# The second pass of the attention scores as two 64-row products on the two halves of the array, in the first half's attention

## The chip, the cores and the metric

The kernel runs on one core of one Trainium2 chip. The metric is the device time of one execution in microseconds; smaller is better. The profile is one execution of the same program, recorded by the hardware profiler.

## The reference

A backbone of two layers over 1024 latent tokens and 256 context tokens, with 1024 features, all in float32. Layer 0 mixes tokens by a convolution module, layer 1 by attention with 16 query heads, 4 key heads and 64 dimensions per head; each is followed by a SwiGLU feed-forward. The part that the change touches:

```python
def gqa_sdpa(q, k, v):
    B, Q, H, Dh = q.shape
    qg = q.reshape(B, Q, N_KV_HEADS, KV_GROUP, Dh)
    s = jnp.einsum("bqkgd,bskd->bkgqs", qg, k).astype(jnp.float32) * (Dh ** -0.5)
    p = jax.nn.softmax(s, axis=-1).astype(v.dtype)
    o = jnp.einsum("bkgqs,bskd->bqkgd", p, v)
    return o.reshape(B, Q, H * Dh)
```

There are 1280 keys (1024 latent and 256 context tokens) and 1024 queries.

## The kernel before

The kernel is one instruction stream per engine, in an order that a scheduler makes from the program's order, its priorities and its tiles. Products run on TensorE in the type float32r, which keeps fewer bits than float32. To keep accuracy, operands are split in two: a high part, rounded to float32r, and a low part, the rest. A projection then takes three products per block (`mm3`, L172 to L174: high by high, high by low, low by high). A weight is split when it is loaded (`wload`, a ScalarE cast and a subtraction).

Attention works in units: one key head t and 128 queries, so four query heads share the keys. 16 units are the first half's attention (queries 0 to 511) and 16 the second's. The first half begins beside the rest of the query projections, then runs alone; the second half runs beside the output projection and the feed-forward.

- `load_q` brings a unit's q from DRAM, where the projections left it, into one of two places of the tile q, on GpSimd's queue (POOL). Its 128 rows are the 64 dimensions of the high part and below them the 64 of the low part. It is called for the next unit when a unit begins.
- `load_k` brings the keys of a head: row block 0 to 63 and row block 64 to 127 hold the same keys; columns 0 to 1279 hold their high part and columns 1280 to 2559 their low part. Heads 0 and 2 lie in the tile KB, heads 1 and 3 in the tile T3 (in `order` rows T_12365).
- `scores` computes, for each of the four query heads, 128 queries by 1280 keys in PSUM. The 1280 columns fall on three banks of 512 columns, as pieces of 512, 512 and 256 (in that order or with the 256 first). Each piece takes two passes of all 128 rows (L1012): (high + low of q) by high of k, then (high + low of q) by low of k, added up in the bank. VectorE scales the piece of 1280 columns and finds its extreme (L1018), ScalarE takes the exponential (L1020).
- `values` transposes the weights by TensorE (L1030), splits them (L1033 on ScalarE, L1034 on VectorE), and multiplies by the values (L1036, L1037), for ten blocks of 128 keys; four more transposes (L1051) bring the sums into place for the division. The weights of one unit are worked on while the scores of the next are made.
- `attn_stream` interleaves the two, and `attention` sets the banks: `sring` says where in PSUM the next head's scores go, one place while projections run beside, two places in turn when attention runs alone.

Scores for a head are followed in program order by some blocks of the unit before; the scheduler moves single products apart from their neighbours where it expects waits, so that the last pieces of a head can stand twenty and more instructions behind the first.

Of the kernel before, what the change touches and what calls it, by code (L numbers as in the profile page):

```python
# [8 lines left out]
F32 = mybir.dt.float32  # L9
F32R = mybir.dt.float32r  # L10
# [5 lines left out]
P = 128  # L16
# [4 lines left out]
TOK = CTX + SEQ  # L21
# [3 lines left out]
NH, NKV, HD = 16, 4, 64  # L25
# [30 lines left out]
class Kern:  # L56
# [936 lines left out]
    def load_q(self, t, qt):  # L993
        nc = self.nc
        self.qi += 1
        q = self.qroom[:, self.qi % 2 * 512:self.qi % 2 * 512 + 512]
        q = q.rearrange("p (h t) -> p h t", h=4)
        nc.gpsimd.dma_start(q, self.qsd[t].rearrange("(r h) t -> r h t", h=4)[:, :, qt * P:(qt + 1) * P])
        return q.bitcast(F32R)

    def scores(self, q, rq, kt, slots, Ps, sums):

        nc = self.nc
        for h in range(4):
            o = self.sring[self.si % len(self.sring)]
            self.si += 1
            sc = self.ps.rearrange("p b n -> p (b n)")[:, o:o + TOK]
            k0 = 0
            while k0 < TOK:
                w = min(512 - (o + k0) % 512, TOK - k0)  # L1010
                for p in range(2):
                    nc.tensor.matmul(sc[:, k0:k0 + w], lhsT=q[:, h, :], rhs=kt[:, p * TOK + k0:p * TOK + k0 + w],  # L1012
                                     start=p == 0, stop=p == 1)
                k0 += w

            mn = self.sp.tile([P, 8], F32, tag="mn", name="mn", bufs=4)[:, 0:1]
            pt = slots[h]
            nc.vector.tensor_scalar(out=pt, in0=sc, scalar1=rq[:, h:h + 1], scalar2=None, op0=ALU.mult, op1=ALU.min,  # L1018
                                    accum_out=mn)
            nc.scalar.activation(pt, pt, AF.Exp, bias=mn, scale=-1.0, accum_out=sums[:, 0, h:h + 1])  # L1020
            Ps.append(pt)
            yield 1.07
# [276 lines left out]

    def attention(self, final, qr):  # L1300
        nc, a, c = self.nc, self.a, self.c
        kbuf = self.T("T3", [P, 2 * TOK], F32R)
        pr1 = self.T("T1", [P, 3, TOK])
        prh = self.T("HS", [P, 4, TOK])
        ptt = self.T("T2", [P, 4, 2, 512], F32R)
# [1 line left out]
        self.ptslot = self.si = self.qi = 0  # L1307
        del self.raws[2:]
        self.qroom = self.room()
        units = [(t, q) for t in range(NKV) for q in range(4)]  # L1310
        self.olast = self.cp.tile([P, 2, P], F32, tag="olast", name="olast")

        def dst(q0):
            def of(t, q):
                if (t, q % 4) == (NKV - 1, 3):
                    return self.olast, lambda: None
                st = self.sb(256).rearrange("p (a q) -> p a q", q=P)

                def done():
                    nc.gpsimd.dma_start(self.od[:, 2 * t:2 * t + 2, q * P:(q + 1) * P], st)  # L1320
                return st, done
            return of
# [9 lines left out]
        self.lav = 40  # L1332
        self.bgq.append(qr)
        pr4 = None
        for us in self.attn_stream(units, (self.kub, kbuf), dst(0), True):
            if self.bgq:
                self.pump(self.rate * us)
            elif pr4 is None:
                pr4 = self.T("T5", [P, 3, TOK])
                self.pring = self.pring[:4] + [pr4[:, 0], pr4[:, 1], pr4[:, 2]] + self.pring[4:]  # L1340
                self.set_banks(**alone)
                self.sring = [0, TOK]
        self.lav = 40

        self.lo_dve = 1.0
        self.set_banks(mm=[6], st=[6], pt=[5], av=[7])
# [116 lines left out]
        for us in self.ffn(1, [(fR[0], 512)], ("T1",), ("HS",), (zR,), parts=2, tail=(first, second)):  # L1463
# [3 lines left out]
            if len(zR) == 1 and not end:  # L1467
# [3 lines left out]
                for j in range(2):  # L1471
                    nc.tensor.matmul(s0[:, j:j + 1], lhsT=yacc[:, j * P:(j + 1) * P], rhs=c["ones"],
                                     start=True, stop=True)
# [100 lines left out]
```

## Time and profile before

| what | value |
|---|---|
| median of 3 runs | 2965.94 us (2965.63 to 2966.03) |
| span of the profiled execution, first to last instruction | 2962.1 us |
| time of that execution outside its span | not on the page; the runs' median is 3.8 us above the span |
| TensorE busy | 2881.8 us, 97% |
| VectorE busy | 1917.6 us, 65% |
| ScalarE busy | 1210.5 us, 41% |
| score products (L1012), both halves | 768 |
| first half's attention | 1578.8 to 1855.0 us |

How to read it: PE is TensorE's products and PEld its weight loads, which run beside products; DVE is VectorE, ACT is ScalarE, POOL is GpSimd. A product's record is longer than its share of TensorE's time, because its modelled end includes the way through the array, where the next product already follows; the distance from start to start is what it costs in a row of products. A row of the order of time has the start and the length in us, engine, line, operation, out<-in, rows*columns of the weights, and rows x columns of the result. A window row has its length, then each engine's busy time and instructions, TensorE's granted clock, and the DMA's share and rate.

### The profile page before, as it was taken

The numbers are of one execution on the slowest core, as the hardware profiler recorded it, in microseconds if no ns is written. First come the engines' busy times: TensorE is split into PE (matmuls) and PEld (weight loads), VectorE is DVE, ScalarE is ACT, GpSimd is POOL, SyncE is SP. The second block draws the span as 40 slices with busy tenths as digits, with TensorE's granted clock in tenths as the row PEclk, the third lists the DMA queues.
The fourth block names the chain that finished last, engine by engine and source line by source line (L and its number), as shares of the span: only waits on it lengthen the run. The fifth ranks groups of instructions, "written<-read, shape, count | busy, mean of one in ns | idle before, by whom it ended". The sixth has DMA issues, their size and how long they took to land.

```text
span 2962.1 us, 38911 instructions
## 1 busy us (share of the span) xinstructions
PE 2881.8 (97%) x14950; PEld 2400.4 (81%) x14950; DVE 1917.6 (65%) x3306; ACT 1210.5 (41%) x2001; POOL 223.2 (8%) x377
## 2 busy tenths in 40 slices
PE   7999989999999999999999999989999999999998
PEld 6888877888888888888878787767777778788887
DVE  6887887857555367334576899786666657543335
ACT  5222265532222135222345788645555543332223
POOL 0000001011122010000011111100000000000000
PEclk9999999999999999999999999999999999999999
DMA  6443434334355234322445211322213143433222
GB/s 246 134 123 97 122 129 172 112 115 136 127 168 173 66 121 157 100 93 92 147 155 162 63 49 45 107 79 79 84 58 87 58 139 97 162 128 100 93 89 76
DMA packets 131449, 336.34 MB, mean 114 GB/s; under 512 B 31296, under 2 KB 52832, under 8 KB 130112
## 3 DMA queue, kind: packets, MB, share of 16 engines
q1 hardware_dynamic: 77728, 222.33, 23.4%
q0 software_dynamic: 29344, 103.83, 10.8%
q10 hardware_dynamic: 24192, 7.70, 1.1%
q8 instruction: 117, 1.92, 0.3%
q14 instruction: 68, 0.56, 0.1%
HBM read 289.50 MB, written 38.93 MB: 111 GB/s over the span
## 4 chain that ended last, share of the span: by engine, by line
PE 89%; DVE 6%; issue 2%; DMA 1%; ACT 1%; POOL 0%; SPq 0%; DVEq 0%; ACTq 0%; POOLq 0%
PE ps L172 20%; PE ps L173 20%; PE ps L174 20%; PE ps L1012 4%; PE ps L1030 4%; PE ps L451 2%; PE ps L453 2%; PE ps L452 2%; PE ps L1036 2%; PE ps L1037 2%; PE ps L184 2%; PE ps L183 2%; PE ps L185 2%; PE ps L529 1%; PE ps L662 1%
## 5 line engine op out<-in xcount | busy, mean ns | idle before, releaser
L174 PE MATMUL ps<-T,wl 128*128 128x512 f32 (+1 forms) x2032 | 766.0, 377 | 3.0 <-DVE wl L148 3.0
L172 PE MATMUL ps<-T,wh 128*128 128x512 f32 (+1 forms) x2032 | 768.1, 378 | 0.5 <-DVE sm L806 0.4
L173 PE MATMUL ps<-T,wh 128*128 128x512 f32 (+1 forms) x1984 | 747.0, 377 | 0.1
L144 ACT CAST wh<-wr 128x1024 fp32r<-128x1024 f32 (+1 forms) x290 | 301.6, 1040 | 734.3 <-PE ps L173 532.6
L148 DVE TENSOR_TENSOR wl<-wr,wh 128x1024 fp32r<-128x1024 f32 (+1 forms) x290 | 351.0, 1211 | 307.9 <-ACT wh L144 303.5
L174 PEld LDWEIGHTS ps<-T,wl 128*128 128x128 f32 x2032 | 384.6, 189 | 72.6 <-DVE wl L148 3.5
L172 PEld LDWEIGHTS ps<-T,wh 128*128 128x128 f32 x2032 | 384.5, 189 | 70.0 <-ACT T L1375 1.7
L173 PEld LDWEIGHTS ps<-T,wh 128*128 128x128 f32 x1984 | 375.6, 189 | 67.3 <-DVE T L164 1.4
L1034 DVE TENSOR_TENSOR T<-ps,T 128x512 fp32r<-128x512 f32 x320 | 216.9, 687 | 108.6 <-ACT T L1033 107.8
L1033 ACT CAST T<-ps 128x512 fp32r<-128x512 f32 x320 | 186.0, 586 | 191.4 <-PE ps L1030 177.7
L173 PE MATMUL ps<-HS,wh 128*128 128x512 f32 x656 | 257.2, 392 | 0.0
L172 PE MATMUL ps<-HS,wh 128*128 128x512 f32 x608 | 238.5, 392 | 0.0
L174 PE MATMUL ps<-HS,wl 128*128 128x512 f32 x608 | 237.7, 391 | 0.0
L1030 PE MATMUL ps<-cst,T 128*128 128x128 f32 x1100 | 189.6, 275 | 3.1 <-DVE T L1034 3.1
L1018 DVE TENSOR_SCALAR_CACHE_REDUCE T<-ps,rq 128x1280 f32<-128x1280 f32 x110 | 170.1, 1546 | 27.8 <-PE ps L1012 22.1
L812 DVE TENSOR_TENSOR sm<-sm,ps 128x256 f32<-128x256 f32 (+1 forms) x88 | 54.6, 620 | 184.1 <-PE ps L174 184.0
L1030 PEld LDWEIGHTS ps<-cst,T 128*128 128x128 f32 x1100 | 132.9, 141 | 49.3 <-DVE T L1034 30.3
L829 DVE TENSOR_TENSOR T<-ps,T 128x512 f32<-128x512 f32 (+1 forms) x168 | 110.6, 663 | 95.4 <-PE ps L174 89.8
L1020 ACT ACTIVATE T<-T,mn 128x1280 f32<-128x1280 f32 x110 | 150.3, 1366 | 38.5 <-DVE T L1018 38.1
L1012 PE MATMUL ps<-KB,q 128*128 128x512 f32 (+1 forms) x576 | 145.1, 370 | 5.3 <-DVE HS L1018 3.1
L173 PEld LDWEIGHTS ps<-HS,wh 128*128 128x128 f32 x656 | 123.4, 188 | 24.0
L1037 PE MATMUL ps<-T,HR 128*128 128x512 f32 x320 | 138.4, 433 | 0.0
(306 smaller groups left out, 4776.1 us busy)
## 6 DMA issues: line engine op xcount, KB each, us to landing
wr<-in_w SPq DMA_DIRECT2D x200, 512.0 KB, 3.4
q<-in_w SPq DMA_DIRECT2D x40, 512.0 KB, 3.5
wr<-in_pw SPq DMA_DIRECT2D x35, 512.0 KB, 3.6
HR<-in_wmodT POOLq DMA_DIRECT2D x56, 256.0 KB, 3.9
q<-in_wmodT POOLq DMA_DIRECT2D x56, 256.0 KB, 4.1
q<-qsd POOLq DMA_DIRECT2D x32, 256.0 KB, 3.3
wr<-in_wo SPq DMA_DIRECT2D x16, 512.0 KB, 3.4
qsd<-T POOLq DMA_DIRECT2D x14, 512.0 KB, 4.2
```

The lines of the kernel that those rows point to most:

```text
L144: nc.scalar.copy(hi, raw)
L148: nc.vector.tensor_tensor(lo, raw, hi.bitcast(F32), op=ALU.subtract)
L172: nc.tensor.matmul(out[:, :n], lhsT=wh, rhs=xh, start=k == 0, stop=False)
L173: nc.tensor.matmul(out[:, :n], lhsT=wh, rhs=xl, start=False, stop=False)
L174: nc.tensor.matmul(out[:, :n], lhsT=wl, rhs=xh, start=False, stop=k == nk - 1)
L1012: nc.tensor.matmul(sc[:, k0:k0 + w], lhsT=q[:, h, :], rhs=kt[:, p * TOK + k0:p * TOK + k0 + w], start=p == 0, stop=p == 1)
L1018: nc.vector.tensor_scalar(out=pt, in0=sc, scalar1=rq[:, h:h + 1], scalar2=None, op0=ALU.mult, op1=ALU.min, accum_out=mn)
L1020: nc.scalar.activation(pt, pt, AF.Exp, bias=mn, scale=-1.0, accum_out=sums[:, 0, h:h + 1])
L1030: nc.tensor.transpose(tp[:, h * P:(h + 1) * P], Ps[h][:, j * P:(j + 1) * P], c["ident"])
L1033: nc.scalar.copy(ph, tp)
L1034: nc.vector.tensor_tensor(pl, tp, ph.bitcast(F32), op=ALU.subtract)
L1037: nc.tensor.matmul(av, lhsT=self.vst[:, t, j, :], rhs=pl, start=False, stop=j == NJ - 1)
```

## The change

In the first half's attention the second pass of a head changes for its two 512-column pieces. The first passes stay. Instead of a second pass of all 128 rows, the piece that comes first takes a product of rows 0 to 63 of q (the high part) with rows 0 to 63 of the low keys, and the other piece takes rows 64 to 127 of a second copy of q's high part with rows 64 to 127 of the low keys. The 256-column piece keeps its two whole passes. The product of the low part of q with the low part of k is left out for the 512-column pieces. The second copy, q2, lies behind the keys in the tile T3, which grows by 1024 columns, and is brought by one more transfer per unit. In the second half `q2` is None and the products are those of before.

```diff
+        src = self.qsd[t].rearrange("(r h) t -> r h t", h=4)[:, :, qt * P:(qt + 1) * P]
+        nc.gpsimd.dma_start(q, src)
+        if self.q2 is None:
+            return q.bitcast(F32R), None
+        q2 = self.q2[self.qi % 2]
+        nc.gpsimd.dma_start(q2.bitcast(F32)[HD:], src[:HD])
+        return q.bitcast(F32R), q2
...
+            k0, half = 0, 0
+            while k0 < TOK:
+                w = min(512 - (o + k0) % 512, TOK - k0)
+                nc.tensor.matmul(sc[:, k0:k0 + w], lhsT=q[:, h, :], rhs=kt[:, k0:k0 + w], start=True, stop=False)
+                if w < 512 or q2 is None:
+                    nc.tensor.matmul(sc[:, k0:k0 + w], lhsT=q[:, h, :], rhs=kt[:, TOK + k0:TOK + k0 + w],
+                                     start=False, stop=True)
+                k0 += w
             k0 = 0
             while k0 < TOK:
                 w = min(512 - (o + k0) % 512, TOK - k0)
-                for p in range(2):
-                    nc.tensor.matmul(sc[:, k0:k0 + w], lhsT=q[:, h, :], rhs=kt[:, p * TOK + k0:p * TOK + k0 + w],
-                                     start=p == 0, stop=p == 1)
+                if w == 512 and q2 is not None:
+                    r = slice(HD * half, HD * half + HD)
+                    qh = (q, q2)[half]
+                    half += 1
+                    nc.tensor.matmul(sc[:, k0:k0 + w], lhsT=qh[r, h, :], rhs=kt[r, TOK + k0:TOK + k0 + w],
+                                     start=False, stop=True)
                 k0 += w
...
-        kbuf = self.T("T3", [P, 2 * TOK], F32R)
+        kbuf = self.T("T3", [P, 2 * TOK + 2 * 4 * P], F32R)
...
+        self.q2 = [kbuf[:, o:o + 4 * P].rearrange("p (h t) -> p h t", h=4) for o in (2 * TOK, 2 * TOK + 4 * P)]
```

The scheduler orders the products anew. The names below: KB and T_12365 are keys (T_12365 also holds q2), q is q, T_12366, T_12865, T_12869 and HS are weights to be transposed, cst is the identity, T_12368 are split weights and HR the values. In the changed program the lines of before L1030, L1036, L1037, L1043 and L1051 are L1047, L1053, L1054, L1060 and L1068, the load of q is L999 and that of q2 L1003; L1017 and L1019 are whole passes and L1029 is a 64-row product.

TensorE, in the part that runs alone, a head of key head 2, before:

```order
L1036 MATMUL ps<-T_12368,HR 128x512
L1012 MATMUL ps<-KB,q 128x512 x2
L1012 MATMUL ps<-KB,q 128x256 x2
L1012 MATMUL ps<-KB,q 128x512 x2
L1030 MATMUL ps<-cst,T_12366 128x128
L1030 MATMUL ps<-cst,T_12865 128x128 x3
```

Six passes of all rows stand between the values' products and the transposes.

The same place after the change:

```order
L1053 MATMUL ps<-T_12368,HR 128x512
L1017 MATMUL ps<-KB,q 128x512 x2
L1017 MATMUL ps<-KB,q 128x256
L1019 MATMUL ps<-KB,q 128x256
L1029 MATMUL ps<-KB,q 128x512
L1029 MATMUL ps<-KB,T_12365 128x512
L1047 MATMUL ps<-cst,T_12366 128x128
L1047 MATMUL ps<-cst,T_12869 128x128 x3
```

The two 64-row products stand side by side at the end, which is so for 33 of the 64 heads.

TensorE, in the part that runs alone, the last two heads of a unit of key head 1, before:

```order
L1012 MATMUL ps<-T_12365,q 128x512 x3
L1030 MATMUL ps<-cst,HS 128x128
L1030 MATMUL ps<-cst,T_12366 128x128
L1030 MATMUL ps<-cst,HS 128x128
L1030 MATMUL ps<-cst,T_12366 128x128
L1012 MATMUL ps<-T_12365,q 128x512
L1012 MATMUL ps<-T_12365,q 128x256 x2
L1012 MATMUL ps<-T_12365,q 128x512
L1051 MATMUL ps<-cst,sb 128x128 x2
```

Here the fourth 512-column pass of a head is held back behind four transposes.

The same place after the change:

```order
L1017 MATMUL ps<-T_12365,q 128x512 x2
L1029 MATMUL ps<-T_12365,q 128x512
L1047 MATMUL ps<-cst,HS 128x128
L1047 MATMUL ps<-cst,T_12366 128x128
L1047 MATMUL ps<-cst,HS 128x128
L1047 MATMUL ps<-cst,T_12366 128x128
L1029 MATMUL ps<-T_12365 128x512
L1017 MATMUL ps<-T_12365,q 128x256
L1019 MATMUL ps<-T_12365,q 128x256
L1017 MATMUL ps<-T_12365,q 128x512
L1068 MATMUL ps<-cst,sb 128x128 x2
```

The two 64-row products stand apart, each between work of the whole array; with other distances (1 to 38 instructions) this is so for 31 heads. Outside the first half's attention every engine's order is that of before.

More of the change, by code (lines that the diff above doesn't have):

```diff
@@ L997, in load_q, with scores @@
         q = q.rearrange("p (h t) -> p h t", h=4)
-        nc.gpsimd.dma_start(q, self.qsd[t].rearrange("(r h) t -> r h t", h=4)[:, :, qt * P:(qt + 1) * P])
-        return q.bitcast(F32R)
-    def scores(self, q, rq, kt, slots, Ps, sums):
+        src = self.qsd[t].rearrange("(r h) t -> r h t", h=4)[:, :, qt * P:(qt + 1) * P]
[5 more added lines that the diff above has]
+        return q.bitcast(F32R), q2
+    def scores(self, qq, rq, kt, slots, Ps, sums):
         nc = self.nc
+        q, q2 = qq
         for h in range(4):
@@ L1334, in attention @@
         pr4 = None
-        for us in self.attn_stream(units, (self.kub, kbuf), dst(0), True):
+        for us in self.attn_stream(units, (self.kub, kbuf[:, :2 * TOK]), dst(0), True):
             if self.bgq:
@@ L1343, in attention @@
         self.lav = 40
+        self.q2 = None
         self.lo_dve = 1.0
```

## The prediction

> **What bounds the kernel now.** First the page's head, for the engine that is busiest and the engine on the chain that ended last.
>
> ```profile
> span 2962.1 us, 38911 instructions
> PE 2881.8 (97%) x14950; PEld 2400.4 (81%) x14950; DVE 1917.6 (65%) x3306; ACT 1210.5 (41%) x2001; POOL 223.2 (8%) x377
> PE 89%; DVE 6%; issue 2%; DMA 1%; ACT 1%; POOL 0%; SPq 0%; DVEq 0%; ACTq 0%; POOLq 0%
> ```
>
> TensorE bounds the kernel as a whole. Only the first half's attention changes, so next the windows over that stage: the part beside the projections, two parts in which it turns to running alone and runs alone, and its end. The 64 heads' scores run from 1578.85 to 1846 us.
>
> ```profile
> core 0: us, PE busy (x) PEld busy (x) DVE busy (x) ACT busy (x) POOL busy (x), PEclk, DMA share, GB/s
> 1578.80:1640.00 61.20, 58.49 (x310) 47.57 (x309) 44.97 (x90) 33.83 (x48) 6.63 (x10) 1.00 0.48 156
> 1640.00:1683.74 43.74, 39.58 (x223) 31.17 (x224) 39.29 (x70) 33.61 (x56) 7.47 (x12) 0.96 0.28 79
> 1683.74:1831.18 147.44, 143.56 (x865) 117.75 (x864) 134.55 (x221) 119.76 (x201) 20.77 (x33) 1.00 0.17 46
> 1831.18:1855.00 23.82, 23.14 (x141) 18.71 (x140) 20.21 (x35) 18.25 (x32) 5.64 (x9) 1.00 0.14 38
> ```
>
> The third row holds five repetitions of the same eight heads (two units of four), 29.5 us each. TensorE is busy 28.7 us of each, VectorE 26.9. So TensorE time added here is paid nearly in full, while of time taken away VectorE lets at most 29.5 - 26.9 = 2.6 us per eight heads through. What TensorE waits for in the stage:
>
> ```profile
> PE ps L1012 <- DVE HS L1018: 5.5, 8, 1.1
> PE ps L1012 <- DVE T L1018: 3.5, 9, 0.8
> PE ps L1030 <- DVE T L1034: 1.6, 1, 1.6
> PE ps L1036 <- ACT T L1033: 0.8, 2, 0.4
> ```
>
> Scores wait for VectorE's read of the bank before them (L1018), 9 us in all; no DMA is waited for. The pace of the products comes from the order of time in the part that runs alone:
>
> ```profile
> 1727.75 0.39 PE L1037 MATMUL ps<-T,HR 128*128 128x512 f32 x1
> 1727.98 0.39 PE L1036 MATMUL ps<-T,HR 128*128 128x512 f32 x1
> 1728.21 0.27 PE L1030 MATMUL ps<-cst,HS 128*128 128x128 f32 x1
> 1728.32 0.27 PE L1030 MATMUL ps<-cst,T 128*128 128x128 f32 x1
> 1728.43 0.27 PE L1030 MATMUL ps<-cst,HS 128*128 128x128 f32 x1
> ```
>
> Start to start, a 512-column product costs 0.23 us and a transpose 0.11; the 0.39 and 0.27 include a tail under which the next one already runs.
>
> **What the change removes.** Per head two 512-column second passes, 2 x 0.23 = 0.46 us, become two 64-row products of the same 512 columns. Only if these run side by side is anything saved. Counted over the whole built order, the 128 products stand as 33 adjacent pairs and 62 single ones with whole-array work on both sides: 95 visits to the half-array arrangement. A single one saves nothing, since it streams the same 512 columns.
>
> What does a visit cost? No 64-row product is in this trace, but L247 is a transpose of 2 rows that the built program places on a 32-row part of the array, among whole-array products:
>
> ```profile
> 52.51 0.28 PE L451 MATMUL ps<-T,wh 128*128 128x256 f32 x1
> 52.63 0.28 PE L452 MATMUL ps<-T,wh 128*128 128x256 f32 x1
> 52.75 0.28 PE L453 MATMUL ps<-T,wl 128*128 128x256 f32 x1
> 52.96 0.22 PE L247 MATMUL ps<-cst,sm 2*128 2x2 f32 x1
> 53.11 0.39 PE L451 MATMUL ps<-T,wh 128*128 128x256 f32 x1
> 53.33 0.28 PE L452 MATMUL ps<-T,wh 128*128 128x256 f32 x1
> ...
> 45.11 0.40 PE L451 MATMUL ps<-T,wh 128*128 128x512 f32 x1
> 45.44 0.27 PE L242 MATMUL ps<-T,cs 128*2 128x128 f32 x1
> ```
>
> These 256-column products start 0.12 us apart. Into L247 it is 0.21: 0.09 more. In the last two rows, from a 512-column product into a 2-column part of the array, it is 0.33 where 0.23 is usual: 0.10 more. I take 0.095 us for a change of arrangement, either way. Then the product behind L247 takes 0.39 instead of 0.28, and its successor starts 0.22 behind it instead of 0.12. The weight loads show why:
>
> ```profile
> 52.63 0.19 PEld L453 LDWEIGHTS ps<-T,wl 128*128 128x128 f32 x1
> 52.96 0.13 PEld L247 LDWEIGHTS ps<-cst,sm 2*128 2x128 f32 x1
> 53.11 0.19 PEld L451 LDWEIGHTS ps<-T,wh 128*128 128x128 f32 x1
> 53.22 0.19 PEld L452 LDWEIGHTS ps<-T,wh 128*128 128x128 f32 x1
> 53.33 0.19 PEld L453 LDWEIGHTS ps<-T,wl 128*128 128x128 f32 x1
> ```
>
> A load normally starts with the product before it; here L247's and L451's waited until the array was empty, and 0.11 us of such a load is exposed. For a transpose's load it is less:
>
> ```profile
> 18.51 0.43 PE L378 MATMUL ps<-cst,nr 128*128 128x128 f32 x2 [0.32 <-DVE nr L350]
> ```
>
> Two transposes at pace take 0.11 + 0.27 = 0.38; this pair, started without a load ahead, took 0.43: 0.05 exposed.
>
> - Entries: 95 x (0.095 + 0.11) = 19.5 us. What follows a first 64-row product needs a full load too.
> - Exits: 95 x 0.095 = 9.0. In the built order 52 exits go to transposes or other short loads, 52 x 0.05 = 2.6, and 43 to full products, 43 x 0.11 = 4.7. Together 16.3.
> - Pairs: the second product can start when its weights are in. Loads start 0.11 us apart above, so I let the two overlap but for 0.11: 0.12 saved per pair, 33 x 0.12 = 4.0. The ends are 0 (one behind the other) and 0.23 (wholly side by side, 7.6); 0.12 is the only spacing that the rows show.
>
> TensorE's work grows by 19.5 + 16.3 - 4.0 = 31.8 us. The ends for a visit are 0 (64 rows change no arrangement) and 0.41 (two full exposures, no overlap: 39 us in all). The nearest rows, the detour over L247, cost 0.58 us from L453 to L452 where two steps of 0.12 would do, 0.34 for one visit; so the upper part is likely.
>
> By the Trainium skill, "TensorEngine Tiling (Array Packing)", section "Tiling Modes", changing the tiling mode, not just the tile, drains TensorE; no run here shows that for 64 rows, but the rows of L247 show it for 32. By "TensorE: Matmul & The Clock Gate", section "Part 3: Packing small matmuls — row/col tiling", products on different rows start about 4 ns apart; no run here shows it, and with that the pairs' 4.0 us would be 7.5 and my time 3.5 us lower.
>
> **What hides part of it.** With TensorE slower by a tenth here, VectorE and ScalarE run less behind, and TensorE's waits shrink. In a repetition TensorE idles 29.5 - 28.7 = 0.8 us by the record. By the paces its work is 8 x (2 x 0.12 + 4 x 0.23) = 9.3 for scores, 20 key chunks x (4 x 0.11 + 2 x 0.23) = 18.0, and 0.4 for four more transposes: 27.7, so up to 1.8 us is slack. I take 0.8 per eight heads, 6.4 us for 64 heads; ends 0 and 14.4.
>
> **What else moves.** Each unit gets a second load of q from DRAM, 64 rows, on POOL's queue: 16 more.
>
> ```profile
> 1702.71 0.77 POOL L998 DMA_DIRECT2D q<-qsd  x1 [3.82 <-PE ps L1012]
> 1713.60 0.75 POOL L998 DMA_DIRECT2D q<-qsd  x1 [10.12 <-PE ps L1012]
> ...
> q<-qsd POOLq DMA_DIRECT2D x32, 256.0 KB, 3.3
> ```
>
> Issuing takes 0.77 us on a queue that is busy 20.8 of 147.4 us, and landing 3.3; it is fetched one unit (14.7 us) ahead. In seven units of the built order the new load stands ahead of q's own, and both wait for the scores of the unit before; q then leaves some 0.8 us later. Queued behind them are the store of the attention output, the small copy for the division (L1043) and, in three places, half of the next keys, which are wanted one to three units later. I cost it at nothing; were the unit's lead gone, each unit would wait up to 0.77 + 3.3 us, 65 us in all. Before, no row shows TensorE waiting for q. The order of the first passes moves too: both 512-column ones now stand ahead of the second passes; they read the same q and keys and keep the same waits on VectorE, so I give that no price. The keys' tile grows, and the built order carries no wait between its old part and the new one. The low half of q times the low half of k is no longer computed, which only leaves rows of the array idle. The order outside this stage is that of before on every engine, SP's queue included.
>
> Sum: 31.8 - 6.4 = 25.4 us on the profiled execution's 2962.1. The page gives no time around that span; the runs' median of 2965.94 lies 3.8 us above it. Forecast 2962.1 + 25.4 + 3.8 = 2991.3, 0.86% slower.
>
> **Rivals.**
> - *Only the emptying costs, the loads go ahead.* If the half-array loads can be put in while the array still works, a visit costs 2 x 0.095: 18.1 - 4.0 - 6.4 = 7.7, 2974. Against it: L451 behind L247 shows the exposed load. For it: its own load is 64 rows, not 128.
> - *No overlap, no slack.* The pairs run one behind the other and the waits on L1018 stay, because they come from the order of banks: 19.5 + 16.3 = 35.8, 3002. For it: TensorE's waits in the alone part are short (at most 1.1 us) and tied to single banks.
> - *Faster or level: no change of arrangement for 64 rows.* Then only the pairs count: -4.0 to -7.6 us of TensorE's work, which VectorE's 2.6 us per eight heads lets through: 2958 to 2962. It decides from a visit's price of 4.0/95 = 0.04 us downwards, a tenth of what L247 shows. Against it speak all rows above; for it, that 32 rows or 2 columns are not 64 rows of 128 columns.
>
> **How the numbers follow.** Forecast 0.61 (2982 to 2998), no overlap and no slack 0.16 (2998 to 3006), only the emptying 0.14 (2968 to 2982), no change of arrangement 0.07, something slower still (a late q) 0.02. The range 2968 to 3004 leaves out the last two and the top of the second. 0.2% is 5.9 us, about what a measurement of this kernel can tell from no change: faster by more than that 0.04, within it 0.06 (the rest of the side-by-side case and the low end of "only the emptying"), slower 0.90.
>
> **What would show it.** In the changed profile: the 64-row products' starts 0.33 us behind a 512-column product instead of 0.23; the whole-array product behind them with a longer record (0.50 instead of 0.39); weight loads of both starting with their own product, not with the one before; a period of eight heads near 32.7 us, with VectorE's busy time still 26.9. Single products at 0.23 on both sides would make the forecast wrong downwards; new waits of TensorE on q's load would make it wrong upwards.

## The result, and the profile after

The changed kernel takes 2987.70 us (median of 4 runs, 2986.62 to 2988.82), the kernel before 2965.99 us beside it (4 runs, 2965.63 to 2967.03). The ratio is 1.0075, with a 95% interval of 1.0061 to 1.0090: 21.7 us slower. Forecast were 25.4 us, and a range that holds the result. The span of the profiled execution is 2985.5 us; in the runs listed with both numbers the time lies 2.0 us above the span. For the kernel before it is 1.8 in the runs of the experiments, so 2 of the prediction's 3.8 us mean that its profiled execution was faster than the median; the forecast difference does not hang on it.

The page after:

```profile
span 2985.5 us, 38936 instructions
PE 2912.6 (98%) x14950; PEld 2400.8 (80%) x14950; DVE 1920.9 (64%) x3306; ACT 1210.5 (41%) x2001; POOL 232.5 (8%) x393
PE 90%; DVE 5%; DMA 2%; issue 1%; ACT 1%; ACTq 0%; POOL 0%; SPq 0%; DVEq 0%; POOLq 0%
```

TensorE's busy time grew by 31 us with the same number of products; VectorE's grew by 3 us, and ScalarE's did not change. The windows of the part that runs alone (the clock is 1.00 in all of them), first three repetitions of eight heads before, then the same three after (columns: length, busy time of PE, PEld, DVE, ACT and POOL, granted clock, DMA share and rate):

```profile
1683.40:1771.63 88.23, 85.90 (x516) 70.52 (x516) 80.48 (x132) 71.51 (x121) 12.09 (x19) 1.00 0.16 43
```

```profile
1694.19:1789.99 95.80, 94.85 (x516) 68.62 (x517) 81.96 (x132) 71.64 (x121) 15.76 (x25) 1.00 0.17 47
1694.19:1726.10 31.91, 31.59 (x173) 22.87 (x173) 27.27 (x44) 23.89 (x41) 4.62 (x7) 1.00 0.11 34
1726.10:1758.03 31.93, 31.61 (x172) 22.88 (x173) 27.34 (x45) 23.86 (x41) 5.49 (x9) 1.00 0.30 75
1758.03:1789.99 31.96, 31.64 (x172) 22.87 (x173) 27.34 (x45) 23.89 (x41) 5.65 (x9) 1.00 0.11 33
```

A repetition takes 31.93 us instead of 29.41. TensorE is busy in 31.6 of it and VectorE in 27.3, so TensorE bounds this part more than before. Counted from the same product before to the same product behind the stage, the stage is 23.8 us longer (283.9 to 307.7) and the rest of the kernel no longer.

What the 64-row products do stands in the order of time after. A single one, and a pair:

```profile
1733.65 0.40 PE L1054 MATMUL ps<-T,HR 128*128 128x512 f32 x1
1733.98 0.50 PE L1029 MATMUL ps<-T 64*128 64x512 f32 x1
1734.41 0.50 PE L1053 MATMUL ps<-T,HR 128*128 128x512 f32 x1
1734.75 0.27 PE L1047 MATMUL ps<-cst,HS 128*128 128x128 f32 x1
...
1736.89 0.28 PE L1019 MATMUL ps<-T,q 128*128 128x256 f32 x1
1737.11 0.50 PE L1029 MATMUL ps<-T,q 64*128 64x512 f32 x1
1737.11 0.50 PE L1029 MATMUL ps<-T 64*128 64x512 f32 x1
1737.54 0.33 PE L1047 MATMUL ps<-cst,HS 128*128 128x128 f32 x1
1737.70 0.27 PE L1047 MATMUL ps<-cst,T 128*128 128x128 f32 x1
```

Into the single product it is 0.33 us where 0.23 is usual, out of it 0.43, and the product behind it takes 0.50 instead of 0.39. From L1054 to the transpose behind L1053 are 1.10 us for three products that would take 0.69 in a row. The pair starts at one time (3 or 4 ns apart in all 33 pairs) and lasts as long as one. The weight loads at the same places:

```profile
1733.42 0.19 PEld L1054 LDWEIGHTS ps<-T,HR 128*128 128x128 f32 x1
1733.98 0.18 PEld L1029 LDWEIGHTS ps<-T 64*128 64x128 f32 x1 [0.37 <-issue]
1734.41 0.19 PEld L1053 LDWEIGHTS ps<-T,HR 128*128 128x128 f32 x1 [0.24 <-ACT T L1050]
...
1737.10 0.18 PEld L1029 LDWEIGHTS ps<-T,q 64*128 64x128 f32 x1
1737.11 0.18 PEld L1029 LDWEIGHTS ps<-T 64*128 64x128 f32 x1
1737.53 0.14 PEld L1047 LDWEIGHTS ps<-cst,HS 128*128 128x128 f32 x1 [0.24 <-issue]
```

In this trace every load into another arrangement starts with its own product, never ahead of it; the two loads of a pair run beside each other, not 0.11 us apart. Over all 95 visits the medians are 0.094 us more than the pace into a visit, 0.11 us of exposed load and 0.09 us on the way out, then 0.056 us (transpose, 51 times) or 0.11 us (product) of the next load. What TensorE waits for in the stage now:

```profile
PE ps L1017 <- DVE HS L1035: 3.0, 8, 0.7
PE ps L1029 <- DMA T<-qsd: 2.1, 1, 2.1
PE ps L1017 <- DVE T L1035: 1.0, 2, 0.7
```

The waits for VectorE's reads of the scores fell from 9.0 to 4.0 us. A wait of 2.1 us for the first unit's second load of q is new.

### The profile page after: what moved, and what is told of

It is laid out like the page before. It is cut to its first block, busy times and chain, and to the rows that moved or that the text cites. A ratio compares the mean times of both kernels' runs of the same rounds, so it can differ in the third digit from the quotient of the medians.

```text
span 2985.5 us, 38936 instructions
## 1 busy us (share of the span) xinstructions
PE 2912.6 (98%) x14950; PEld 2400.8 (80%) x14950; DVE 1920.9 (64%) x3306; ACT 1210.5 (41%) x2001; POOL 232.5 (8%) x393
## 4 chain that ended last, share of the span: by engine, by line
PE 90%; DVE 5%; DMA 2%; issue 1%; ACT 1%; ACTq 0%; POOL 0%; SPq 0%; DVEq 0%; POOLq 0%
PE ps L172 20%; PE ps L174 20%; PE ps L173 20%; PE ps L1047 4%; PE ps L1053 2%; PE ps L451 2%; PE ps L1054 2%; PE ps L453 2%; PE ps L452 2%; PE ps L1017 2%; PE ps L184 2%; PE ps L183 2%; PE ps L185 2%; PE ps L1019 1%; PE ps L529 1%
## 5 line engine op out<-in xcount | busy, mean ns | idle before, releaser
L1051 DVE TENSOR_TENSOR T<-ps,T 128x512 fp32r<-128x512 f32 x320 | 216.9, 688 | 113.6 <-ACT T L1050 112.1
L1047 PE MATMUL ps<-cst,T 128*128 128x128 f32 x1100 | 192.9, 277 | 2.3 <-DVE T L1051 2.3
L1035 DVE TENSOR_SCALAR_CACHE_REDUCE T<-ps,rq 128x1280 f32<-128x1280 f32 x110 | 170.1, 1546 | 31.9 <-PE ps L1019 21.7
L1047 PEld LDWEIGHTS ps<-cst,T 128*128 128x128 f32 x1100 | 132.4, 142 | 48.7 <-DVE T L1051 27.8
L1037 ACT ACTIVATE T<-T,mn 128x1280 f32<-128x1280 f32 x110 | 150.3, 1366 | 39.9 <-DVE T L1035 39.3
L1053 PE MATMUL ps<-T,HR 128*128 128x512 f32 x320 | 137.0, 428 | 2.9 <-ACT T L1050 2.9
L1054 PE MATMUL ps<-T,HR 128*128 128x512 f32 x320 | 139.3, 435 | 0.0
```

The costliest lines, as they stand in the source:

```text
L1047: nc.tensor.transpose(tp[:, h * P:(h + 1) * P], Ps[h][:, j * P:(j + 1) * P], c["ident"])
L1051: nc.vector.tensor_tensor(pl, tp, ph.bitcast(F32), op=ALU.subtract)
L1053: nc.tensor.matmul(av, lhsT=self.vst[:, t, j, :], rhs=ph, start=j == 0, stop=False)
L1054: nc.tensor.matmul(av, lhsT=self.vst[:, t, j, :], rhs=pl, start=False, stop=j == NJ - 1)
```

## The experiments

The theory: the price hangs on visits. A visit to the half-array arrangement costs 0.30 us (0.094 + 0.11 + 0.09) and the next load's exposure; two products side by side save 0.227 us; a part of the sum goes into TensorE's slack (the visits' 35.8 us less 7.5 for the pairs are 28.3 us of work; measured are 21.7, so 6.6 went there). Rivals: the second load of q, the new order of passes, or a price per 64-row product. In the kernels with 64-row products the low part of q times the low part of k is left out there, as in the change. The differences below are between medians, beside the kernel before on the same chip.

**Both products on the same half.** No pair runs side by side, and the second load of q is gone.

```diff
-        q2 = self.q2[self.qi % 2]
-        nc.gpsimd.dma_start(q2.bitcast(F32)[HD:], src[:HD])
-        return q.bitcast(F32R), q2
+        return q.bitcast(F32R), q.bitcast(F32R)
...
-                    r = slice(HD * half, HD * half + HD)
+                    r = slice(0, HD)
```

> The change, but both 64-row products of a head use rows 0 to 63 of the array, with q's own high rows, and the second load of q is gone; 93 visits, 35 of them with two products. Theory (a visit costs about 0.38 us: 0.094 into it, 0.11 and 0.11 or 0.056 of exposed weight loads, 0.095 out of it; two products side by side save 0.227): work grows by 93 x 0.296 + 53 x 0.056 + 40 x 0.11 = 34.9 us, less the 6.6 us of slack that the changed kernel recovered: 28 us slower than before, 6 slower than the change. Rival 1 (the second load of q or its wait is the cost): near before, within 5 us. Rival 2 (side by side is worth nothing, because weight loads pace it): as the change, 21 to 23 us slower than before.

Measured: 2989.44 us against 2964.85, ratio 1.0076 (1.0057 to 1.0094), 24.6 us slower. That rules out the load of q as the cause, for it is absent. It is 3 us below the 28 that were expected, and the times alone don't tell it from the change: the traced run of this kernel also has 23.9 us of the stage at half the clock (granted clock 0.5), against 13.7 in the first record of the change. The trace does: the products of a pair now start 0.34 us apart, and the repetition of eight heads takes 32.27 us (96.82 / 3) with TensorE never idle:

```profile
1694.85:1791.67 96.82, 96.82 (x518) 70.25 (x517) 81.83 (x132) 71.72 (x122) 12.00 (x19) 1.00 0.15 39
```

So side by side is worth 4 x 0.227 = 0.91 us per eight heads in work, but only 0.34 of it in time; the rest would have come out of slack. That fits the waits: TensorE waits for VectorE's reads of the scores 0.3 us in this kernel's stage, 4.0 in the change and 9.0 before.

**The load and the order alone.** The second passes are whole products again; the load of q2 and the order of the passes stay.

```diff
-                    nc.tensor.matmul(sc[:, k0:k0 + w], lhsT=qh[r, h, :], rhs=kt[r, TOK + k0:TOK + k0 + w],
+                    nc.tensor.matmul(sc[:, k0:k0 + w], lhsT=q[:, h, :], rhs=kt[:, TOK + k0:TOK + k0 + w],
```

> The change's second load of q and its order of passes, but the second passes of the 512-column pieces are whole products of 128 rows, as before. Theory: no visit, so within 3 us of before. Rival (the load, POOL's queue or the order of passes cost): 10 to 20 us slower than before.

Measured: 2965.57 against 2964.85, ratio 1.0004 (0.9995 to 1.0013). Neither the load, POOL's queue nor the order of passes costs anything that can be measured here; the interval goes from 1.5 us faster to 4 us slower. (Nothing waits for the load in this kernel, so the 2.1 us above are not covered by it.)

**One 64-row product per head.** The other second pass is whole; 64 visits, no pair.

```diff
-                    r = slice(HD * half, HD * half + HD)
+                    r = slice(0, P if half else HD)
```

(and no second load of q, as in the first experiment)

> Of each head one second pass is a 64-row product and the other a whole one; no second load of q; 64 visits with one product each, nothing side by side. Theory: 64 x 0.296 + 43 x 0.11 + 21 x 0.056 = 24.8 us of work, less 6.6 of slack: 18 us slower than before. Rival (the price hangs on the count of 64-row products, 128 in the change, 64 here): half of the change's, 11 us slower. Rival (the load or the order): 0.

Measured: 2980.14 against 2964.85, ratio 1.0048 (1.0033 to 1.0063), 15.3 us slower: between the theory's 18 and the 11 of a price per product, and the interval (10 to 19 us) holds both. The repetition speaks against a price per product:

```profile
1689.86:1783.20 93.34, 93.34 (x518) 70.52 (x516) 81.38 (x132) 72.10 (x122) 12.05 (x19) 1.00 0.14 40
```

31.11 us, 1.70 more than before. Eight visits by the theory add 3.1 us of work, and the change's twelve with four pairs 3.6 for 2.52 more in time. A price per product would give half of 2.52, 1.26. How much of the 3.1 goes into slack is not known ahead, so 1.70 does not confirm the theory's sum by itself; the prices in the order of time and the runs with more pairs below carry it.

**The second half's attention instead.** There dense projections run beside it. Same half, no second load; the first half as before.

```diff
-        self.q2 = [kbuf[:, o:o + 4 * P].rearrange("p (h t) -> p h t", h=4) for o in (2 * TOK, 2 * TOK + 4 * P)]
+        self.q2 = None
...
-        self.q2 = None
+        self.q2 = True
```

(with the edits of the first experiment)

> The first half's attention as before; in the second half's attention, which runs beside the output projection and the feed-forward, the second passes of the 512-column pieces are 64-row products on rows 0 to 63; 76 visits, 52 of them with two products one behind the other. Theory: 76 x 0.296 + 30 x 0.056 + 46 x 0.11 = 29.3 us, with little slack to recover where dense projections run beside: 26 to 29 us slower than before. Rival (half-array visits cost what TensorE waits for anyway, so a denser stage hides more or as much): 22 us or less.

Measured: 2988.39 against 2964.85, ratio 1.0079 (1.0064 to 1.0094), 23.5 us slower, between the two expectations. The stage's own length grew by 23.9 us for 29.3 us of work. The waits that the two traces list there (from 1855 to 2545 us) did not shrink, 12.1 and 12.7 us. But an estimate by the paces of the trace before (1712 products at 0.229 us, 701 at 0.109, 128 at 0.118, 24 at 0.112) gives some 486 us of work for a stage of 518.9, so there is more room than the listed waits. Which of it took the other 5.4 us is not shown. The interval, 19 to 28 us, holds both expectations.

**The pairs kept together by priority.** The scores' products get 200 steps of priority in the first half; 62 of 64 pairs stand together, 66 visits. Its yardstick is the kernel before with the same priority.

```diff
+            self.tc.cur_priority -= 200 if q2 is not None else 0
             while k0 < TOK:
...
+            self.tc.cur_priority += 200 if q2 is not None else 0
```

> The change, with the scores' products given a higher priority in the first half's attention (200 steps), so that the two 64-row products of a head stand side by side for 62 heads of 64; 66 visits. Theory: 66 x 0.296 + 58 x 0.056 + 8 x 0.11 = 23.6 us, less 62 x 0.227 = 14.1 saved: work grows by 9.5 us, less up to 6.6 of slack: 3 to 9 us slower than the kernel before with the same priority. Rival (the price is per product, not per visit): 20 us or more slower, as the change. Rival (once all pairs stand together the change pays): level or faster than the kernel before with the same priority.

> The kernel before with the same higher priority for the scores' products in the first half's attention and nothing else: the yardstick of the run with the pairs together. The order alone moves no work: within 4 us of before.

Measured: 3000.39 us, and 2986.74 for the yardstick, against 2964.65; ratios 1.0114 (1.0100 to 1.0127) and 1.0074 (1.0060 to 1.0088). The yardstick's expectation failed: the priority alone costs 22 us. A part of it is that score products now stand in TensorE's queue where their bank is not yet read (columns: total, times, longest):

```profile
PE ps L1014 <- DVE T L1021: 7.8, 14, 1.1
PE ps L1014 <- DVE HS L1021: 6.3, 13, 0.8
```

That is 14.1 us instead of 9.0, so these waits explain 5 of the 22 us. Another part is the clock: in its record 20.5 us around the stage run at half the clock, against 6.8 before. The rest is open. Beside it the pairs cost 13.7 us more, above the 3 to 9 expected and below the 20 of a price per product. The intervals of the two are some 4 us wide each way, so the sign is sure and the size is not. The record shows 2.2 us of it: the first unit waits for the second load of q here too.

**The products of two heads behind the first passes of both.** A gentler way to more pairs: where attention runs alone, the 64-row products of two heads are issued behind both heads' first passes; 71 visits, 56 pairs. The yardstick has whole products in the same order of issue.

```diff
+            held.append((h, o, sc))
+            batch = q2 is not None and len(self.sring) == 2
+            for g, o, sc in ([] if batch and h % 2 == 0 else held):
+                k0, half = 0, 0
...
+                        qh = (q, q2)[half]
+                        nc.tensor.matmul(sc[:, k0:k0 + w], lhsT=qh[r, g, :], rhs=kt[r, TOK + k0:TOK + k0 + w],
+                                         start=False, stop=True)
```

> The change, but where attention runs alone the 64-row products of two heads are issued behind the first passes of both, so that more pairs stand together: 71 visits instead of 95, 56 pairs side by side instead of 33. Theory: 71 x 0.297 + 24 x 0.11 + 47 x 0.056 - 56 x 0.227 = 13.7 us more work than the same order with whole products, of which up to 9 may be slack: 5 to 14 us slower than that one, against some 22 for the change beside the kernel before. Rival (the price goes with the count of 64-row products): 20 us or more beside it.

> The same order of issue as in the run with two heads together, with whole products of 128 rows in place of the 64-row ones: its yardstick. VectorE reads two heads one behind the other, so a wait or two per unit may come in: 0 to 10 us slower than before.

Measured: 2984.42 us, and 2974.66 for the yardstick, against 2963.63; ratios 1.0071 (1.0059 to 1.0084) and 1.0033 (1.0021 to 1.0045). Beside its yardstick it is 9.8 us slower, where the change is 21.7: as expected, with the same 128 products and 24 visits fewer. The three repetitions, first of the yardstick, then of this kernel:

```profile
1685.53:1777.86 92.33, 85.54 (x518) 69.16 (x516) 80.94 (x133) 72.77 (x121) 12.42 (x20) 1.00 0.15 41
1691.85:1785.74 93.89, 88.32 (x517) 65.84 (x516) 81.75 (x133) 72.72 (x121) 16.10 (x26) 1.00 0.18 48
```

TensorE's busy time grows by 0.9 us per eight heads, where it grew by 3.0 in the change. So the smaller price is less work, and not only work hidden under more waits. The kernel is slower than the one before nonetheless, since the order itself costs 11 us. No version that beats the kernel before came out of this: even a pair in every visit leaves 0.30 + 0.056 - 0.227 = 0.13 us per visit on the wrong side. Two pairs in one visit would gain 0.10 us by the same prices, but no kernel was made of such visits. The single one in this trace (at 1858.62 us) gained nothing: 0.79 us pass from its first product to the transpose behind it, 0.94 with the way in and the transpose's load, against 0.92 for four whole products. One case does not settle it.

**The change once more**, for a second record.

> The changed kernel once more, for a second record of it: whether the 13.6 us at half the clock in the stage and the 2.1 us wait for the second load of q come back. Theory: the wait does, since it is set by the order; the half clock comes back if the change causes it, and differs if it is a matter of where the clock's windows fall.

Measured: one time of 2983.46 us. The repetition is 31.94 us again:

```profile
1690.88:1786.69 95.81, 94.86 (x516) 68.62 (x516) 81.92 (x132) 71.58 (x121) 15.71 (x25) 1.00 0.17 47
```

But the 2.1 us wait did not come back. I had expected it to, as set by the order; it hung on the transfer instead: the first load of q2 took 6.6 us from issue to landing in the first record and 4.1 here. The stage is 4.4 us shorter (303.3), all of it ahead of the part that runs alone. TensorE runs at half the clock for 10.2 us of the stage here, 13.7 in the first record and 4.5 before. These are single records, so what part of it the change causes stays open. The 64-row products are not needed for it, as the 20.5 us around the stage in the kernel with the priority alone show.

## Why the prediction was right, step by step

For eight heads in the part that runs alone, with the prices from the trace after (0.297 per visit; 0.056 or 0.11 for the next load; 0.227 saved per pair) and 27.7 us of work before:

| kernel | visits | pairs | work added | repetition | longer than its yardstick |
|---|---|---|---|---|---|
| before | 0 | 0 | 0 | 29.41 | |
| change | 12 | 4 | 3.6 | 31.93 | 2.52 |
| same half | 12 | 0 | 4.5 | 32.27 | 2.86 |
| one 64-row product | 8 | 0 | 3.1 | 31.11 | 1.70 |
| two heads together, whole | 0 | 0 | 0 | 30.77 | |
| two heads together | 8 | 8 | 1.1 | 31.30 | 0.53 |
| the load and the order alone | 0 | 0 | 0 | 29.45 | 0.04 |
| priority, whole | 0 | 0 | 0 | 31.61 | |
| pairs together by priority | 8 | 8 | 1.0 | 33.06 | 1.45 |

The last row is the one that does not fit: it is longer by more than the work added. Its three repetitions are uneven (34.1, 32.4 and 32.7 us), and why is not shown. In the other rows with 64-row products the time is shorter than the work, by what the slack takes.

- The visit's price, taken from a 2-row transpose (0.095 in, 0.11 load, 0.095 out, 0.05 or 0.11 next load), was right to 0.01 us each for 64 rows. This step carries the forecast. As the prediction had asked, a 64-row product starts 0.33 us behind a 512-column one, the product behind it has a record of 0.50, and its load starts with it. The rule of the Trainium skill, "TensorEngine Tiling (Array Packing)", section "Tiling Modes", that a change of tiling mode drains TensorE, fits what the trace shows for 64 rows: 0.094 us more than the pace at the entry.
- The pairs' term was mis-sized: 0.12 us saved each, 4.0 in all, where 0.227 was there, 7.5 in all. The loads do not take turns when their rows differ. The sentence with the 4 ns of the Trainium skill, "TensorE: Matmul & The Clock Gate", section "Part 3: Packing small matmuls — row/col tiling", was nearer: 3 or 4 ns here.
- The slack was mis-sized too: 0.8 us per eight heads was the recorded idle; 3.6 - 2.52 = 1.1 was recovered in the change and up to 1.65 in the same-half kernel, of the 1.7 that the paces left. Recorded idle time of TensorE is too small by the tail of each record, as the second way of counting in that step said.
- With both: 35.8 - 7.5 - 8 x 1.1 = 19.5 us, near the 8 x 2.52 = 20.2 that the repetition gives for 64 heads. Ahead of the repetitions lie 40 of the 128 products, 6.3 us at that price. From the last product that both orders share to the first repetition, the first record is 11.1 us longer than before and the second 6.6. The 4.5 us between the two records hold the wait for q of 2.1 us, which I had costed at nothing, and 3.5 us more at half the clock, of which about half is lost.
- So the two mis-sized terms put the forecast 5.9 us too high, and a wait and a clock that the prediction did not price seem to have made up some 2 us of it. That the forecast came as near as 3.7 us is in that part luck.
- Against "only the emptying costs" stand the exposed loads; against "no overlap, no slack" the pairs at 3 or 4 ns and the waits that fell to 4.0 us; against "no change of arrangement" every entry.
- "A period near 32.7" was 31.9, which follows from the two terms above. "VectorE still 26.9" was 27.3; what the 0.4 us are is not shown.

## What to carry to other kernels

Half-array products pay only if what they save in one visit is more than the way in and out: here 0.35 to 0.40 us, against 0.23 for one pair of 512 columns. Before splitting products to run side by side, look in the built order whether they stand side by side; a scheduler that fills in other work between them turns one visit into two. And where a saving or a cost lands on an engine with a little idle time, count its work from the paces, not from the idle time that the record shows.

## What the runs showed of the hardware

- Two 64-row products on different halves start 3 or 4 ns apart with their weight loads beside each other, and the second costs nothing: 0.43 us from the first to what follows, as for a single one.
- Two 64-row products on the same half, one behind the other, start 0.34 us apart, 0.11 more than whole-array products. The 0.11 is the exposed load of the first one; the second one's load is taken ahead. From the trace of the second half's attention in the fourth kernel (the two products are merged in the second row, and their two loads in the last):

```profile
2100.31 0.62 PE L1015 MATMUL ps<-KB,q 128*128 128x512 f32 x2
2100.86 0.74 PE L1027 MATMUL ps<-KB,q 64*128 64x512 f32 x2
2101.53 0.50 PE L1051 MATMUL ps<-T,HR 128*128 128x512 f32 x1
...
2100.86 0.29 PEld L1027 LDWEIGHTS ps<-KB,q 64*128 64x128 f32 x2 [0.36 <-issue]
```

Both loads are over 0.29 us behind the start of the first product, while the second product starts 0.34 behind it. From L1027 to L1051 are 0.67 us, 0.24 more than for a pair on two halves: the second product costs no more than its pace, so the way in, the load and the way out are paid once per visit and not once per product.

- At half the clock a 512-column product takes 0.427 us from start to start instead of 0.229, in every kernel's record; within the stage such stretches came in steps of 3.4 us, and it held 4.5 to 24 us of them. One begins between 1638 and 1653 us in every record, where the attention turns to running alone; beyond that these runs explain no pattern.
